# A mixture of experts in 26 units instead of 28: wide experts share a unit with a narrow one

## The chip, the cores and the metric

The kernel runs on one core of a Trainium2 chip. The metric is the time of one execution on the device in microseconds, the median of several runs. The engines are named as the profile names them: PE is the matrix engine TensorE (PEld its weight loads), DVE is VectorE, ACT is ScalarE, POOL is GpSimd, and SP is the engine whose queue issues nearly all DMAs here.

## The reference

Two transformer blocks run one after the other on 256 tokens of width 1024. The first has a pooling mixer, an attention layer and two dense feed-forward layers; the second has a gated recurrent mixer and then a mixture of 64 experts. The change concerns the mixture and, in one detail, the dense feed-forward layers.

```python
def moe_ffn(h, w_router, b_router, w_gu, w_down, w_sh_gu, w_sh_down):
    scores = jax.nn.sigmoid((h @ w_router).astype(jnp.float32))
    sel = scores + b_router
    ...                                   # keep the best 4 of 8 groups of experts
    _, top_e = lax.top_k(sel, TOP_K)      # 8 experts for each of 256 tokens
    w = jnp.take_along_axis(scores, top_e, axis=1)
    w = w / jnp.sum(w, axis=-1, keepdims=True) * ROUTED_SCALE
    ...
    out = swiglu_2(h_pad[tok], w_gu[e], w_down[e])   # per expert, on its own tokens
    acc = acc.at[tok].add(out * wts[:, None])
    ...
    return acc[:N] + swiglu_2(h, w_sh_gu, w_sh_down)
```

An expert is a gate-and-up product (1024 to 2 x 256), a SiLU gate, and a down product (256 to 1024), all in float32. 256 tokens times 8 choices are 2048 token slots over 64 experts; how many each expert gets depends on the data.

## The kernel before

**Weights.** An expert's weights are three pieces of 128 x 2048 float32 (1024 KB): the gate and up rows of the first and of the second half of the 1024 inputs, and the down rows. `load_experts` issues them on SP, L1735, for all experts of a unit piece by piece: first pieces of every expert, then second, then third. The pieces live in a ring of 17 buffers (`NEX` = 11 and `NEX2` = 6). A load waits until the matmuls have read what its buffer held before. Before the routed experts SP also loads three pieces of the shared expert.

**Units.** The core computes experts in units. A unit fills the 128 columns of TensorE's stationary operand with token slots, and the string `UNITS` gives the order:

```python
NFIX = 8
UNITS = "FFFFSSMHMSMMHMSMMHMSMMMHSMMM"
ROOM = {"F": (2, 64), "H": (1, 128), "M": (2, 64), "S": (4, 32)}
```

An F unit holds two given experts (the last eight by number, 56 to 63), with 64 slots each. The other 56 experts are ranked by their number of tokens: the 4 largest get an H unit each with 128 slots, the next 28 share 14 M units with 64 slots each, the 24 smallest share 6 S units with 32 slots each. The position in the string is the position in time. An expert with more tokens than slots has the rest done in a loop at the end (L1910), two entries at a time.

**The plan.** F units need no routing result for their loads, since their experts are given. For the others `placement` computes on the core which expert has which rank and writes the numbers into a small table, `plan` (L1644). SP reads the numbers of a unit's experts from it (`entry`, L1741), one read for each expert, and only then issues that unit's loads. `load_unit` and `loads` only set the order in SP's queue. The table has one column for each block of slots, `NCOL` = 60 in all.

**A unit's work.** For two neighbouring units `gather` (L1792) multiplies the tokens by a 0/1 matrix made by `onehot`; its result `xg` holds the units' tokens as columns. `front` (L1809) runs over the 8 blocks of 128 inputs, and for each over the experts of the unit; each expert has its own strip of output rows. Its first four blocks read the first piece of each expert, the last four the second. SiLU on ACT (L1812) and the product on DVE (L1814) follow. `back` (L1841) transposes the result and multiplies it by the third piece, in two halves of 512 columns; for each half it takes two steps. `scatter` (L1853) adds the unit's result to the accumulators of the tokens; it stands in the middle of the next unit, between front and back. So a unit frees its buffers at three steps: the middle of the front, the end of the front, the end of the back. Every float32 matmul is two instructions in the trace.

**Small buffers.** The dense feed-forward layers compute their gate in `swiglu`: ACT writes `sil` (L694), DVE multiplies it into `a32`, named `a` in the trace (L696), ACT makes the high part `ah` (L699), and POOL the low part `al` (L700). `sil` and `a32` have two buffers each, and the experts use the same.

Of the kernel before, what the change touches and what calls it, by code (L numbers as in the profile page):

```python
# [20 lines left out]
T = 256  # L21
# [6 lines left out]
NLIST = 32  # L28
NEX = 11
NEX2 = 6  # L30
NFIX = 8
UNITS = "FFFFSSMHMSMMHMSMMHMSMMMHSMMM"
ROOM = {"F": (2, 64), "H": (1, 128), "M": (2, 64), "S": (4, 32)}
NUNIT = len(UNITS)


def column_plan():


    count = {k: UNITS.count(k) * ROOM[k][0] for k in "HMS"}  # L40
    assert sum(count.values()) == N_EX - NFIX and 2 * UNITS[:NFIX // 2].count("F") == NFIX
    at = {"H": 0, "M": count["H"], "S": count["H"] + count["M"]}
    cols, first = [], []
    for k in UNITS[NFIX // 2:]:
        first.append(len(cols))
        for _ in range(ROOM[k][0]):
            cols.extend((at[k], s) for s in range(0, ROOM[k][1], 64))
            at[k] += 1
    return cols, first, count["H"], count["H"] + count["M"]


COLS, FIRST_COL, RANK_M, RANK_S = column_plan()
NCOL = len(COLS)


# [93 lines left out]
class Kern:  # L149
# [540 lines left out]

    def swiglu(self, ps):
        nc = self.nc
        sil = self.small([128, 256], "sil", 2)
        nc.scalar.activation(sil, ps[:, 0:256], AF.Silu)  # L694
        a = self.small([128, 256], "a32", 2)
        nc.vector.tensor_tensor(a, sil, ps[:, 256:512], op=ALU.mult)  # L696
        ah = self.small([128, 1, 256], "ah", TAIL + 1, F32R)
        al = self.small([128, 1, 256], "al", TAIL + 1, F32R)
        nc.scalar.copy(ah[:, 0, :], a)  # L699
        nc.gpsimd.tensor_tensor(al[:, 0, :], a, ah[:, 0, :], op=ALU.subtract)  # L700
        return ah, al
# [201 lines left out]
    def second_ffn(self, p):  # L903
# [11 lines left out]
        def load_x():  # L915
            for c in range(2):
                nc.gpsimd.dma_start(out=cx[:, c, :], in_=A["ctx"][128 * c:128 * c + 128, :])
            self.lower = self.small([128, 128], "lower", 1)
            nc.gpsimd.dma_start(out=self.lower, in_=A["lower"])

        def load_gs():
# [485 lines left out]
    def post(self, ctx, ws_ctx):  # L1407
# [20 lines left out]
        nc.gpsimd.dma_start(out=self.tri8, in_=self.A["tri8"])  # L1428
        self.ei = self.small([64, 4], "ei", 1)
        nc.gpsimd.dma_start(out=self.ei, in_=self.A["eidx"])  # L1430
        self.at = self.small([128, 128], "lower", 1)
        nc.gpsimd.dma_start(out=self.at, in_=self.A["colat"])
        self.loads(3 + NEX - 4)
        hs = [slice(512 * h, 512 * h + 512) for h in range(2)]
# [154 lines left out]
    def shared_expert(self):  # L1589

        nc, w, gu = self.nc, self.wsh, self.gu
        sil, act, aT = [], [], []
        for c in range(2):
            sil.append(self.small([128, 256], "sil", 2))
            nc.scalar.activation(sil[c], gu[c][:, 0:256], AF.Silu)
        for c in range(2):
            act.append(self.small([128, 256], "a32", 2))
            nc.vector.tensor_tensor(act[c], sil[c], gu[c][:, 256:512], op=ALU.mult)
        yield
        for c in range(2):  # L1600
# [12 lines left out]
        self.down = down  # L1613
        yield

    def placement(self):
# [4 lines left out]
        tmp = _Arena(self.small([128, 512], "hx", 3))  # L1621
        t = lambda n: tmp.tile([64, n])
        idx, given, key0 = ei[:, 0:1], ei[:, 2:3], ei[:, 3:4]
        ranks, bases = self.at[0:64, 0:NCOL], self.at[0:64, 64:64 + NCOL]
        n = N_EX - NFIX
        pc = self.pst([64, n + 1])
        for c in range(2):
# [16 lines left out]
        V.tensor_copy(self.plan, pe)  # L1644

        room, less = t(1), t(1)
        V.tensor_scalar(room, rank, RANK_M - 0.5, -64.0, op0=ALU.is_lt, op1=ALU.mult)
        V.tensor_scalar(less, rank, RANK_S - 0.5, 32.0, op0=ALU.is_gt, op1=ALU.mult)
        V.tensor_tensor(less, less, given, op=ALU.mult)
        V.scalar_tensor_tensor(room, room, -64.0, less, op0=ALU.add, op1=ALU.add)  # L1650
# [68 lines left out]
    def load_unit(self, n):  # L1719

        u = n - NFIX // 2
        if u < 0:
            idx = [N_EX - NFIX + 2 * n + e for e in range(2)]
        else:
            idx = self.entry(self.plan, FIRST_COL[u], ROOM[UNITS[n]][0])
        self.ex[n] = [[] for _ in idx]
        yield from self.load_experts(idx, self.ex[n])

# [31 lines left out]
    def experts(self):  # L1760
# [37 lines left out]
                    nc.vector.tensor_copy(xg[:, k0:k0 + 2, 0:m], ps[:, :, 0:m])  # L1798
            return xg, ow

        def front(ws, xg, j, inside={}):

            r, o = 128 // len(ws), 128 * j
            gu = self.psw()
            for k in range(8):
                for f in inside.get(k, ()):
                    f()
                for e, w in enumerate(ws):
                    nc.tensor.matmul(gu[r * e:r * e + r, :], xg[:, k, o + r * e:o + r * e + r],  # L1809
                                     w[k // 4][:, 512 * (k % 4):512 * (k % 4) + 512], start=(k == 0), stop=(k == 7))  # L1810
            sil = self.small([128, 256], "sil", 2)
            nc.scalar.activation(sil, gu[:, 0:256], AF.Silu)  # L1812
            act = self.small([128, 256], "a32", 2)
            nc.vector.tensor_tensor(act, sil, gu[:, 256:512], op=ALU.mult)  # L1814
            return act

        def back(ws, act, ow, j, scatter=lambda c, nb: None):

            r = 128 // len(ws)
# [12 lines left out]
            oT = self.small([128, 2, 128], "ah", TAIL + 1, F32R)  # L1832
            nc.vector.reduce_sum(sw, pt, axis=AX.X)
            nc.vector.tensor_scalar(oT.rearrange("p c t -> p (c t)"), pt, 0.0, None, op0=ALU.is_gt)
            yh = self.per.tile([128, 1024], F32R, tag="acc8", name="yh")
            yl = self.small([128, 1024], "grow", 3, F32R)
            for nb in range(2):
                y = self.psw()
                for f in range(2):
                    for e, w in enumerate(ws):  # L1840
                        nc.tensor.matmul(y[r * e:r * e + r, :], aT[:, f, r * e:r * e + r],  # L1841
                                         w[2][:, 1024 * f + 512 * nb:1024 * f + 512 * nb + 512],
                                         start=(f == 0), stop=(f == 1))
# [45 lines left out]
        for n in range(NUNIT):  # L1889
            ws = self.ex.pop(n)  # L1890
            done += 3 * len(ws)
            if n % 2 == 0:
                grp = gather(*oh, 2)
            act = front(ws, grp[0], n % 2, {} if n else {1: [lambda: next(self.shared)], 3: [lambda: next(side)],
                                                           6: [lambda: next(side)]})
            if n == 0:
                GP2 = self.row(self.rows, 7 * 1024, 1024)
# [4 lines left out]
            pend = scatter(*back(ws, act, grp[1], n % 2, pend))  # L1902
            next(side, None)
            if n == 0:
                self.down(1, 0)
# [5 lines left out]
        with tc.For_i(0, n, 2) as i:  # L1911
            ws = [[], []]
            for _ in self.load_experts(self.entry(self.li, i, 2), ws):
                pass
            grp = gather(*onehot([(self.slotx[:, :, ds(i, 2)], self.Wx[:, :, ds(i, 2)])]), 1)
            all4(scatter(*back(ws, front(ws, grp[0], 0), grp[1], 0)))
# [46 lines left out]
def _prepare(I):  # L1963
# [112 lines left out]
    at = np.zeros((128, 128), f32)  # L2076
    at[:, 0:NCOL] = [r for r, _ in COLS]
    at[:, 64:64 + NCOL] = [-s for _, s in COLS]
    A["colat"] = at
    A["eidx"] = ei  # L2080
    return A
# [14 lines left out]
```

## Time and profile before

| | us |
|---|---|
| median of 3 runs | 1332.54 (1332.06 to 1334.05) |
| the profiled execution, its own time | 1334.75 |
| span of its instructions | 1332.9 |
| PE busy | 1274.2 |
| DVE busy | 646.2 |
| ACT busy | 526.0 |
| POOL busy | 228.3 |

The experts are the last third of the span: their first front starts at 857.0 us. The busy time of PE is an upper figure, since matmuls overlap and their ends are modelled. All loads of expert weights go through one DMA queue, so the moved GB/s in a window and the times at which SP issues its loads say more about a limit there than a share of busy time does.

### The profile page before, as it was taken

The page shows a single profiled execution, that of the slowest core. Times are in us where ns is not written, and L with a number is a line of the kernel's source. Part 1 is how long each engine was busy: PE and PEld are TensorE (multiplying, and loading weights), DVE is VectorE, ACT ScalarE, POOL GpSimd, SP SyncE. Part 2 cuts the span into 40 slices and gives each one's busy share as a digit, 9 for nine tenths or more (in the row PEclk, how much of TensorE's full clock was granted, in tenths as well). Part 3 has the DMA queues.
Part 4 walks back from the last instruction along what each step waited for, and adds up shares of the span by engine and source line. Part 5 has one row for each costly group of instructions (what it writes and reads, how often), then busy time and mean ns, then how long its engine had stood idle before and what let it go on. Part 6 is the DMA issues. An engine that isn't in the chain of part 4 may idle for free. (4 is left out here: it accounts for less than half of the span.)

```text
span 1332.9 us, 20200 instructions
## 1 busy us (share of the span) xinstructions
PE 1274.2 (96%) x7812; PEld 922.1 (69%) x7812; DVE 646.2 (48%) x984; ACT 526.0 (39%) x883; POOL 228.3 (17%) x230
## 2 busy tenths in 40 slices
PE   7999999999999999989988899999998999999986
PEld 5889887988798998878887897544453443534532
DVE  5664555846657456576879557423222222222223
ACT  6534444557554456556645345311111111111112
POOL 1111112123033000125246442200000000000000
PEclk8999999999999999999999999999999999999998
DMA  8768678444485575646434478799999999999994
GB/s 301 252 231 280 248 270 316 155 164 159 130 326 189 189 249 194 221 151 242 143 104 136 152 274 342 273 372 378 405 420 420 419 420 419 420 419 420 421 420 192
DMA packets 72817, 374.45 MB, mean 281 GB/s; under 512 B 8932, under 2 KB 9364, under 8 KB 44304
## 3 DMA queue, kind: packets, MB, share of 16 engines
q1 hardware_dynamic: 68912, 361.25, 71.3%
q0 software_dynamic: 3664, 11.89, 2.8%
q8 instruction: 62, 1.02, 0.3%
q14 instruction: 35, 0.29, 0.1%
q10 hardware_dynamic: 144, 0.01, 0.0%
HBM read 371.99 MB, written 1.11 MB: 280 GB/s over the span
## 5 line engine op out<-in xcount | busy, mean ns | idle before, releaser
L137 DVE TENSOR_TENSOR wlo<-wland,whi 128x1024 fp32r<-128x1024 f32 x201 | 244.2, 1249 | 104.4 <-ACT whi L134 103.6
L258 PE MATMUL pw<-hT,whi 128*128 128x256 f32 x1856 | 250.6, 282 | 0.0
L134 ACT CAST whi<-wland 128x1024 fp32r<-128x1024 f32 x236 | 237.2, 1046 | 25.2 <-PE pa L267 12.7
L258 PEld LDWEIGHTS pw<-hT,whi 128*128 128x128 f32 x1856 | 232.9, 189 | 12.6 <-ACT whi L134 6.5
L1809 PE MATMUL pw<-ex,xg 128*64 128x512 f32 (+2 forms) x1024 | 208.5, 596 | 5.0 <-DMA ex<-ex 4.8
L1809 PEld LDWEIGHTS pw<-ex,xg 128*64 128x64 f32 (+2 forms) x1024 | 65.7, 130 | 133.3 <-issue 107.4
L258 PE MATMUL pw<-hT,wlo 128*128 128x256 f32 x928 | 128.2, 280 | 0.0
L1841 PE MATMUL pw<-ex,al 128*64 128x512 f32 (+2 forms) x512 | 113.2, 613 | 7.9 <-DMA ex<-ex 7.9
L258 PEld LDWEIGHTS pw<-hT,wlo 128*128 128x128 f32 x928 | 117.2, 189 | 0.2 <-POOL wlo L137 0.2
L137 POOL TENSOR_TENSOR wlo<-wland,whi 128x1024 fp32r<-128x1024 f32 x35 | 87.4, 2497 | 162.7 <-ACT whi L134 127.9
L267 PE MATMUL pa<-whi,hT 128*128 128x512 f32 x352 | 114.6, 401 | 0.0
L1814 DVE TENSOR_TENSOR a<-sil,pw 128x256 f32<-128x256 f32 x28 | 11.8, 421 | 190.5 <-ACT sil L1812 190.5
L1846 DVE SCALAR_TENSOR_TENSOR grow<-pw,sw,yh 128x512 fp32r<-128x512 f32 x56 | 42.1, 751 | 111.9 <-ACT yh L1845 111.0
L1812 ACT ACTIVATE sil<-pw 128x256 f32<-128x256 f32 x28 | 10.8, 385 | 209.0 <-PE pw L1809 209.0
L700 POOL TENSOR_TENSOR al<-a,ah 128x256 fp32r<-128x256 f32 x44 | 32.6, 742 | 326.9 <-ACT ah L699 326.9
L1841 PEld LDWEIGHTS pw<-ex,al 128*64 128x64 f32 (+2 forms) x512 | 31.9, 132 | 74.9 <-issue 49.9
L1845 ACT ACTIVATE yh<-pw,sw 128x512 fp32r<-128x512 f32 x56 | 38.5, 688 | 111.1 <-PE pw L1841 111.1
L694 ACT ACTIVATE sil<-pw 128x256 f32<-128x256 f32 x44 | 16.9, 384 | 164.7 <-PE pw L258 164.7
L1780 POOL TENSOR_TENSOR grow<-hx,Wp 128x256 f32<-128x256 f32 x24 | 14.7, 630 | 383.7 <-DVE hx L1778 383.7
L267 PEld LDWEIGHTS pa<-whi,hT 128*128 128x128 f32 x352 | 66.5, 189 | 16.1 <-DVE hT L248 0.4
L267 PE MATMUL pa<-wlo,hT 128*128 128x512 f32 x176 | 70.2, 399 | 5.0 <-DVE wlo L137 3.4
L267 PE MATMUL pa<-wlo,ah 128*128 128x512 f32 x176 | 69.8, 397 | 0.5 <-DVE wlo L137 0.5
(400 smaller groups left out, 1780.8 us busy)
## 6 DMA issues: line engine op xcount, KB each, us to landing
ex<-ex SPq DMA_DIRECT2D x192, 1024.0 KB
wland<-wd SPq DMA_DIRECT2D x236, 512.0 KB
ada<-ada SPq DMA_DIRECT2D x24, 1024.0 KB
row<-rows POOLq DMA_DIRECT2D x6, 512.0 KB, 4.9
ex<-exs SPq DMA_DIRECT2D x3, 1024.0 KB
bias<-bscr POOLq DMA_DIRECT2D x4, 512.0 KB, 4.8
x<-x SPq DMA_DIRECT2D x4, 256.0 KB
pw<-poolw SPq DMA_DIRECT2D x2, 512.0 KB
```

The costliest lines, as they stand in the source:

```text
L134: nc.scalar.copy(h, t)
L137: eng.tensor_tensor(l, t, h, op=ALU.subtract)
L258: self.nc.tensor.matmul(out, a[:, o:o + 128], b[:, k, :], start=(p == 0 and k == 0), stop=(p == 2 and k == nk - 1))
L267: self.nc.tensor.matmul(out, a[:, k, cs], b[:, lo:lo + n], start=(first and p == 0), stop=(last and p == 2))
L694: nc.scalar.activation(sil, ps[:, 0:256], AF.Silu)
L700: nc.gpsimd.tensor_tensor(al[:, 0, :], a, ah[:, 0, :], op=ALU.subtract)
L1780: nc.gpsimd.tensor_tensor(view(ow), view(oh), W[:, :, :, None].to_broadcast(shape), op=ALU.mult)
L1809: nc.tensor.matmul(gu[r * e:r * e + r, :], xg[:, k, o + r * e:o + r * e + r], w[k // 4][:, 512 * (k % 4):512 * (k % 4) + 512], start=(k == ...
L1814: nc.vector.tensor_tensor(act, sil, gu[:, 256:512], op=ALU.mult)
L1841: nc.tensor.matmul(y[r * e:r * e + r, :], aT[:, f, r * e:r * e + r], w[2][:, 1024 * f + 512 * nb:1024 * f + 512 * nb + 512], start=(f == 0 ...
L1845: nc.scalar.activation(yh[:, sl], y, AF.Copy, scale=sw)
L1846: nc.vector.scalar_tensor_tensor(yl[:, sl], y, sw, yh[:, sl], op0=ALU.mult, op1=ALU.subtract)
```

## The change

The 4 H units go, and there are 4 T units in their place. A T unit holds one of the 4 largest experts with 96 slots (L) and one small expert with 32 slots (S). With four small experts placed there, and six given experts and not eight, the string becomes 3 F, 6 S, 4 T and 13 M units: 26.

The 96 slots of an L expert are two strips, 64 and 32 columns wide, since a strip starts at a multiple of its width; `strips` lists them. So the front of a T unit has three matmuls for each of 8 blocks where H had one, and the back three for each of its 4 steps. The rooms are 96 for ranks 0 to 3, 64 for ranks 4 to 29 and 32 for the last 28 of 58 ranked experts.

The table of columns grows to `NCOL` = 66, and its tile from 128 to 132 columns. `sil` and `a32` have one buffer each and not two; the shared expert, which needs two at once, takes the second from `ah` and `al`.

```diff
-NFIX = 8
-UNITS = "FFFFSSMHMSMMHMSMMHMSMMMHSMMM"
-ROOM = {"F": (2, 64), "H": (1, 128), "M": (2, 64), "S": (4, 32)}
+NFIX = 6
+UNITS = "FFFSSTMMSTMMSTMMSTMMSMMMMM"
+ROOM = {"F": 64, "L": 96, "M": 64, "S": 32}
+PARTS = {"F": "FF", "M": "MM", "T": "LS", "S": "SSSS"}
...
+        for k in PARTS[u]:
+            own[-1].append(len(cols))
+            cols.extend((at[k], s) for s in range(0, ROOM[k], 64 if u == "M" else 32))
             at[k] += 1
...
+def strips(unit):
+    at, out = 0, []
+    for k in PARTS[unit]:
+        out.append([(at + s, min(64, ROOM[k] - s)) for s in range(0, ROOM[k], 64)])
+        at += ROOM[k]
+    return out
...
     def swiglu(self, ps):
-        sil = self.small([128, 256], "sil", 2)
+        sil = self.small([128, 256], "sil", 1)
-        a = self.small([128, 256], "a32", 2)
+        a = self.small([128, 256], "a32", 1)
...
-        self.at = self.small([128, 128], "lower", 1)
+        self.at = self.small([128, 2 * NCOL], "lower", 1)
...
-            sil.append(self.small([128, 256], "sil", 2))
+            sil.append(self.small([128, 256], ("sil", "ah")[c], (1, TAIL + 1)[c]))
-            act.append(self.small([128, 256], "a32", 2))
+            act.append(self.small([128, 256], ("a32", "al")[c], (1, TAIL + 1)[c]))
...
-        V.tensor_scalar(room, rank, RANK_M - 0.5, -64.0, op0=ALU.is_lt, op1=ALU.mult)
+        V.tensor_scalar(room, rank, RANK_M - 0.5, -32.0, op0=ALU.is_lt, op1=ALU.mult)
...
-            idx = self.entry(self.plan, FIRST_COL[u], ROOM[UNITS[n]][0])
+            idx = [x for c in OWN_COLS[u] for x in self.entry(self.plan, c, 1)]
...
-                for e, w in enumerate(ws):
-                    nc.tensor.matmul(gu[r * e:r * e + r, :], xg[:, k, o + r * e:o + r * e + r],
-                                     w[k // 4][:, 512 * (k % 4):512 * (k % 4) + 512], start=(k == 0), stop=(k == 7))
+                for w, own in zip(ws, strips(unit)):
+                    for s, r in own:
+                        nc.tensor.matmul(gu[s:s + r, :], xg[:, k, o + s:o + s + r],
+                                         w[k // 4][:, 512 * (k % 4):512 * (k % 4) + 512], start=(k == 0), stop=(k == 7))
...
-                    for e, w in enumerate(ws):
-                        nc.tensor.matmul(y[r * e:r * e + r, :], aT[:, f, r * e:r * e + r],
-                                         w[2][:, 1024 * f + 512 * nb:1024 * f + 512 * nb + 512],
-                                         start=(f == 0), stop=(f == 1))
+                    for w, own in zip(ws, strips(unit)):
+                        for s, r in own:
+                            nc.tensor.matmul(y[s:s + r, :], aT[:, f, s:s + r],
+                                             w[2][:, 1024 * f + 512 * nb:1024 * f + 512 * nb + 512],
+                                             start=(f == 0), stop=(f == 1))
```

Three places show what moves. The names are `out<-in` with the tile's shape; `ex` is a piece of an expert's weights. The first place is SP's queue at the end of the loads of given experts, before:

```order
L1735 DMA ex_8312<-ex 128x2048
L1735 DMA ex_8314<-ex 128x2048
L1735 DMA ex_8316<-ex 128x2048
L1735 DMA ex<-ex 128x2048 x11
L1741 TENSOR_LOAD plan
L1741 ISA x2
```

And the same place after the change:

```order
L1748 DMA ex_8312<-ex 128x2048
L1748 DMA ex_8314<-ex 128x2048
L1748 DMA ex_8316<-ex 128x2048
L1748 DMA ex<-ex 128x2048 x5
L1754 TENSOR_LOAD plan
L1754 ISA x2
```

The first of four reads of the plan moved ahead of six loads. The second place is PE at the fourth unit (position 3), before:

```order
L1841 MATMUL pw<-ex,al 64x512 x8
L1701 MATMUL pt<-hx,ei 1x32 x4
L1702 MATMUL pt<-hx,ei 1x1
L1667 MATMUL pt<-cst,sc 64x128 x2
L1809 MATMUL pw<-ex,xg 64x512 x16
```

And after:

```order
L1855 MATMUL pw<-ex,al 64x512 x8
L1714 MATMUL pt<-hx,ei 1x32 x4
L1715 MATMUL pt<-hx,ei 1x1
L1680 MATMUL pt<-cst,sc 64x128 x2
L1823 MATMUL pw<-ex,xg 32x512 x18
```

Where the last F unit had two strips of 64 (16 matmuls), an S unit with four strips of 32 now stands, with its 32 matmuls and twelve loads. The third place is PE at a front with one of the largest experts, before an H unit (position 7):

```order
L1853 MATMUL pa<-grow,ah 128x512
L1841 MATMUL pw<-ex,al 64x512 x8
L1809 MATMUL pw<-ex,xg 128x512 x8
L1853 MATMUL pa<-yh,ah 128x512
L1853 MATMUL pa<-grow,ah 128x512
```

And after, the start of the first T unit's front (position 5), where the last row begins the second block:

```order
L1855 MATMUL pw<-ex_8941,al 32x512
L1823 MATMUL pw<-ex_8963,xg 64x512
L1823 MATMUL pw<-ex_8963,xg 32x512
L1823 MATMUL pw<-ex_8965,xg 32x512
L1823 MATMUL pw<-ex_8963,xg 64x512
```

One matmul over 128 columns became three, over 64 and 32 columns of the large expert (`ex_8963`) and 32 of the small one (`ex_8965`).

## Rows read from the trace of the kernel before

**Rows 1.** The page: GB/s in 40 equal slices; DMA issues, count and size.

```profile
GB/s 301 252 231 280 248 270 316 155 164 159 130 326 189 189 249 194 221 151 242 143 104 136 152 274 342 273 372 378 405 420 420 419 420 419 420 419 420 421 420 192
...
ex<-ex SPq DMA_DIRECT2D x192, 1024.0 KB
```

**Rows 2.** Windows: us, busy (count) of PE, PEld, DVE, ACT, POOL; PEclk, DMA, GB/s.

```profile
898.00:902.00 4.00, 4.00 (x20) 1.29 (x18) 0.00 (x0) 0.00 (x0) 0.00 (x0) 1.00 0.70 225
...
914.00:918.00 4.00, 4.00 (x20) 1.21 (x16) 0.00 (x0) 0.06 (x1) 0.00 (x0) 1.00 0.99 348
918.00:922.00 4.00, 4.00 (x24) 2.91 (x25) 2.07 (x6) 0.69 (x2) 1.22 (x2) 1.00 0.98 377
...
930.00:934.00 4.00, 4.00 (x44) 1.26 (x40) 0.00 (x0) 0.00 (x0) 0.00 (x0) 1.00 0.96 338
934.00:938.00 4.00, 4.00 (x34) 2.01 (x27) 0.56 (x2) 0.38 (x1) 0.00 (x0) 1.00 0.86 350
...
900.00:945.00 45.00, 44.45 (x296) 20.46 (x296) 13.27 (x37) 8.19 (x16) 1.22 (x2) 1.00 0.97 380
945.00:1310.00 365.00, 352.15 (x1814) 162.09 (x1808) 81.55 (x154) 59.86 (x110) 13.44 (x22) 1.00 1.01 420
...
1104.00:1108.00 4.00, 4.00 (x24) 0.98 (x17) 0.00 (x0) 0.61 (x1) 0.00 (x0) 0.57 1.02 424
```

**Rows 3.** Timeline of PE, the last units: start, us, instruction, idle before and its releaser.

```profile
1280.33 3.65 PE L1809 MATMUL pw<-ex,xg 128*64 128x512 f32 x14 [1.33 <-DMA ex<-ex]
...
1289.99 4.16 PE L1792 MATMUL pt<-hx,h 128*128 128x256 f32 x32
1294.08 7.09 PE L1809 MATMUL pw<-ex,xg 128*64 128x512 f32 x32
...
1307.16 7.09 PE L1809 MATMUL pw<-ex,xg 128*64 128x512 f32 x32
...
1316.66 3.65 PE L1841 MATMUL pw<-ex,al 128*64 128x512 f32 x16
...
1320.24 0.51 PE L1853 MATMUL pa<-yh,ah 128*128 128x512 f32 x1
```

**Rows 4.** Timeline of PE: the front of an S unit and of an H unit.

```profile
929.16 7.07 PE L1809 MATMUL pw<-ex,xg 128*32 128x512 f32 x64
...
1060.06 7.03 PE L1809 MATMUL pw<-ex,xg 128*128 128x512 f32 x16
```

**Rows 5.** Timeline of PE: the first front, where 128 columns interrupt 64.

```profile
857.04 1.08 PE L1809 MATMUL pw<-ex,xg 128*64 128x512 f32 x4
858.05 0.66 PE L1603 MATMUL pt<-cst,a 128*128 128x128 f32 x4
```

**Rows 6.** Issues on SP: reads of the plan (ns, starts), then single expert loads.

```profile
L1741 SPq TENSOR_LOAD <-plan x4: 262/268/478, 882.3 to 884.3; - x4
...
865.70 0.33 SPq L1735 DMA_DIRECT2D ex<-ex  x1
881.96 0.33 SPq L1735 DMA_DIRECT2D ex<-ex  x1
885.10 0.35 SPq L1735 DMA_DIRECT2D ex<-ex  x1
899.72 0.33 SPq L1735 DMA_DIRECT2D ex<-ex  x1
...
949.14 0.33 SPq L1735 DMA_DIRECT2D ex<-ex  x1
1295.31 0.33 SPq L1735 DMA_DIRECT2D ex<-ex  x1
```

**Rows 7.** Timeline of DVE: the plan is written.

```profile
863.84 0.21 DVE L1644 CAST plan<-pt 1x60 int32<-1x60 f32 x1 [1.50 <-PE pt L1642]
```

**Rows 8.** Timelines of POOL and DVE in the first feed-forward layer.

```profile
39.46 0.74 POOL L700 TENSOR_TENSOR al<-a,ah 128x256 fp32r<-128x256 f32 x1 [4.13 <-ACT ah L699]
...
44.12 0.42 DVE L696 TENSOR_TENSOR a<-sil,pw 128x256 f32<-128x256 f32 x1 [0.17 <-ACT sil L694]
```

More of the change, by code (lines that the diff above doesn't have):

```diff
@@ L30 @@
 NEX2 = 6
-NFIX = 8
-UNITS = "FFFFSSMHMSMMHMSMMHMSMMMHSMMM"
-ROOM = {"F": (2, 64), "H": (1, 128), "M": (2, 64), "S": (4, 32)}
+NFIX = 6
+UNITS = "FFFSSTMMSTMMSTMMSTMMSMMMMM"
+ROOM = {"F": 64, "L": 96, "M": 64, "S": 32}
+PARTS = {"F": "FF", "M": "MM", "T": "LS", "S": "SSSS"}
 NUNIT = len(UNITS)
 def column_plan():
[L40 to L44, printed above, removed]
+    count = {k: sum(PARTS[u].count(k) for u in UNITS) for k in "FLMS"}
+    assert UNITS[:NFIX // 2] == "F" * (NFIX // 2) and count["F"] == NFIX and sum(count.values()) == N_EX
+    at = {"L": 0, "M": count["L"], "S": count["L"] + count["M"]}
+    cols, first, own = [], [], []
+    for u in UNITS[NFIX // 2:]:
         first.append(len(cols))
-        for _ in range(ROOM[k][0]):
-            cols.extend((at[k], s) for s in range(0, ROOM[k][1], 64))
+        own.append([])
+        for k in PARTS[u]:
+            own[-1].append(len(cols))
+            cols.extend((at[k], s) for s in range(0, ROOM[k], 64 if u == "M" else 32))
             at[k] += 1
-    return cols, first, count["H"], count["H"] + count["M"]
-COLS, FIRST_COL, RANK_M, RANK_S = column_plan()
+    return cols, first, own, count["L"], count["L"] + count["M"]
+def strips(unit):
[4 more added lines that the diff above has]
+    return out
+COLS, FIRST_COL, OWN_COLS, RANK_M, RANK_S = column_plan()
 NCOL = len(COLS)
@@ L917, in load_x @@
                 nc.gpsimd.dma_start(out=cx[:, c, :], in_=A["ctx"][128 * c:128 * c + 128, :])
-            self.lower = self.small([128, 128], "lower", 1)
+            self.lower = self.small([128, 2 * NCOL], "lower", 1)[:, 0:128]
             nc.gpsimd.dma_start(out=self.lower, in_=A["lower"])
@@ L1623, in placement @@
         idx, given, key0 = ei[:, 0:1], ei[:, 2:3], ei[:, 3:4]
-        ranks, bases = self.at[0:64, 0:NCOL], self.at[0:64, 64:64 + NCOL]
+        ranks, bases = self.at[0:64, 0:NCOL], self.at[0:64, NCOL:2 * NCOL]
         n = N_EX - NFIX
@@ L1799, in gather, with front @@
             return xg, ow
-        def front(ws, xg, j, inside={}):
-            r, o = 128 // len(ws), 128 * j
+        def front(ws, unit, xg, j, inside={}):
+            o = 128 * j
             gu = self.psw()
@@ L1807, in front, with back @@
                     f()
-                for e, w in enumerate(ws):
-                    nc.tensor.matmul(gu[r * e:r * e + r, :], xg[:, k, o + r * e:o + r * e + r],
-                                     w[k // 4][:, 512 * (k % 4):512 * (k % 4) + 512], start=(k == 0), stop=(k == 7))
-            sil = self.small([128, 256], "sil", 2)
+                for w, own in zip(ws, strips(unit)):
+                    for s, r in own:
+                        nc.tensor.matmul(gu[s:s + r, :], xg[:, k, o + s:o + s + r],
+                                         w[k // 4][:, 512 * (k % 4):512 * (k % 4) + 512], start=(k == 0), stop=(k == 7))
+            sil = self.small([128, 256], "sil", 1)
             nc.scalar.activation(sil, gu[:, 0:256], AF.Silu)
-            act = self.small([128, 256], "a32", 2)
+            act = self.small([128, 256], "a32", 1)
             nc.vector.tensor_tensor(act, sil, gu[:, 256:512], op=ALU.mult)
             return act
-        def back(ws, act, ow, j, scatter=lambda c, nb: None):
-            r = 128 // len(ws)
+        def back(ws, unit, act, ow, j, scatter=lambda c, nb: None):
             for c, nb in ((0, 0), (0, 1), (1, 0)):
@@ L1893, in experts @@
                 grp = gather(*oh, 2)
-            act = front(ws, grp[0], n % 2, {} if n else {1: [lambda: next(self.shared)], 3: [lambda: next(side)],
+            act = front(ws, UNITS[n], grp[0], n % 2, {} if n else {1: [lambda: next(self.shared)], 3: [lambda: next(side)],
                                                            6: [lambda: next(side)]})
@@ L1901, in experts @@
                 oh = onehot(two(n + 1))
-            pend = scatter(*back(ws, act, grp[1], n % 2, pend))
+            pend = scatter(*back(ws, UNITS[n], act, grp[1], n % 2, pend))
             next(side, None)
@@ L1915, in experts @@
             grp = gather(*onehot([(self.slotx[:, :, ds(i, 2)], self.Wx[:, :, ds(i, 2)])]), 1)
-            all4(scatter(*back(ws, front(ws, grp[0], 0), grp[1], 0)))
+            all4(scatter(*back(ws, "M", front(ws, "M", grp[0], 0), grp[1], 0)))
         self.warm(AF.Sqrt)
@@ L2075, in _prepare @@
     ei[:, 3] = -ei[:, 0] - 1.0e6 * (1.0 - ei[:, 2])
-    at = np.zeros((128, 128), f32)
+    at = np.zeros((128, 2 * NCOL), f32)
     at[:, 0:NCOL] = [r for r, _ in COLS]
-    at[:, 64:64 + NCOL] = [-s for _, s in COLS]
+    at[:, NCOL:] = [-s for _, s in COLS]
     A["colat"] = at
```

## The prediction, made before the changed kernel ran

> **What bounds the kernel now.** I began with the slices of the page. In the last third the moved bytes stand at 419 to 421 GB/s slice after slice, and the page lists 192 expert loads of 1024 KB, which is 64 experts times three [rows 1]. The windows say it more exactly: from 945 to 1310 us the queue moves 420 GB/s without a dip, while from 900 to 945 it moves 380 [rows 2]. One load of 1.049 MB at 420 GB/s is 2.50 us. The issue rows agree: from the load issued at 949.14 to the last one at 1295.31 there are 138 steps in 346.17 us, 2.51 us each [rows 6]. So from 945 us on, the weights bound the kernel, and both kernels load the same 192 pieces.
>
> Then the timeline of TensorE, for what a unit costs it. The last two M units run from the gather at 1289.99 to the scatter that follows them at 1320.24, 30.25 us for a pair (gather 4.16, twice front 7.09, scatter and transposes, back 3.65) [rows 3]. Twelve loads are 30.0 us. So TensorE keeps pace with M units almost exactly, and waits in S units (12 loads in one unit). Just after the last S it waits for a load (1.33 us before the row at 1280.33), and from there to the end it waits for none [rows 3].
>
> The time is therefore: the moment when the queue becomes saturated, plus a fixed amount of loading, plus the TensorE work after the last place where it waited for data. Only the first and the third can change.
>
> **The change, part by part.** The sum is made against the profiled execution: span 1332.9 us, its own time 1334.75; the median is 1332.54, and I apply the difference to that.
>
> *Two units fewer.* 28 units at 30.25/2 = 15.1 us become 26: TensorE has 30.25 us less to do. The loads it waits for cover that fully, so I count nothing. The cover goes only if a unit gets dearer (below).
>
> *The ring frees faster, earlier.* A load needs a place in a ring of 17 pieces, and before 945 us the queue is idle because TensorE has not yet freed places. An F unit frees two at each of its three steps, an S unit four. Position 3 was F and is S now; its releases at about 914, 918 and 925 us free 12 places, 30 us of loading, in place of 6. From 900 to 945 the idle share is 1 - 380/420, that is 4.3 us [rows 2]. Of this the row 914 to 918 gives 0.69 us (348 GB/s), 918 to 922 gives 0.41 (377), 930 to 934 gives 0.78 (338) and 934 to 938 gives 0.67 (350): 2.5 us that I expect to go. The row 898 to 902 (225 GB/s, 1.86 us) lies before the new releases and stays. What idles before 898 belongs to units 0 to 2, which are the same F units.
>
> *Reads of the plan move.* The first load of each routed unit is behind reads of its experts' numbers on SP: four reads, the first at 882.3 and the last at 884.3, stand between the load issued at 881.96 and the next at 885.10, 3.14 us apart where two that need nothing stand some 0.5 apart: 2.6 us [rows 6]. With six given experts these reads stand after 18 expert loads and not 24. The load that went out at 865.70 is now the first one behind them. The plan is written at 863.84, for 0.21 us [rows 7]; 864.05 plus 2.6 is 866.7, so this load is 1.0 us later, in a stretch where places in the ring set the pace. The place in the old order, at 882, loses its 2.6 us in turn. The next S unit has its reads behind the load of 899.72 [rows 6], and the one after it goes out up to 2.3 us later than it did; there the queue is nearly empty (225 GB/s), so this is new idle time. I take a third of it, 0.8, since four loads released by 903 and 910 queue up behind it and part of the lost time was idle anyway; the bounds are 0 and 2.3. Gain at the moment of saturation: 2.5 - 0.8 = **1.7 us**, between 0.2 and 3.4 (4.3 less the half of 1.86 that lies after 900).
>
> *The four T units.* H was one expert with 128 columns, 8 matmuls in the front and 4 in the back. T does 64, 32 and 32 columns as three, so 24 and 12. The trace has no unit of mixed widths. It has three of one width: one 128 strip takes 7.03 us for a front, two 64 strips 7.09, four 32 strips 7.07 [rows 3, 4]. Strips of one width overlap wholly, and the nearest rows say that T costs 7.1 too: nothing extra. The other bound is no overlap: three strips one after the other cost twice more, 2 x (7.09 + 3.65) = 21.5 us, and each change of width something. A change from 64 to 128 columns shows: from four instructions of a 64 pair to the next width it is 1.01 us (857.04 to 858.05), against 4/32 of 7.09 = 0.89 in a steady front [rows 3, 5], 0.12 more. With 24 changes (16 in the front, 8 in the back) that is 2.9, in all 24.4. Between them: the 64 strip alone, the two 32 strips together, 10.7 + 2.9 = 13.6 us. I take 0, but the result is the same up to 14.5: a stretch S T M M has 30 loads, 75.0 us, and four units of TensorE, 60.5. What a T costs below 14.5 us extra goes into waiting that is there anyway.
>
> On this the Trainium skill speaks against the change: its page TensorEngine Tiling (Array Packing), Key Properties, says that changing the tiling mode, and not just the tile, drains TensorE. By that rule the widths would not overlap and the middle or upper case would hold, and the sum would stay as it is or be that of the slower rival; no row before shows widths side by side.
>
> *The end.* After the last S there were three M units and now there are five. In each pair TensorE needs 30.25 and the loads 30.0, so the lag grows by one more 0.25, say **+0.3 us**. That the first of them waits for data as now is what carries this step. Longer waits in S units can lower TensorE's clock: in one S unit that had waited for its loads the granted clock was 0.57 from 1104 to 1108 [rows 2], mostly the lower of its two levels (1.2 and 2.4 GHz). About 4 us at half speed cost 2; where loads are waited for anyway it costs nothing, at the very end up to 2.
>
> *One buffer for sil and a32.* In the first FFN the POOL subtraction that reads a32 runs 39.46 to 40.20, and the next write of a32 starts at 44.12 [rows 8], 3.9 us later, the closest pair of the trace. So the new wait is met already and costs nothing. The wider table, 66 columns and not 60, adds a few columns to instructions of 0.2 us; nothing waits for them.
>
> Sum: -1.7 + 0.3 = -1.4 us, **1331.1 us** against 1332.54, which is -0.1%.
>
> **Rivals.**
> *Slower: widths do not overlap at all.* T costs 24.4 us extra, 9.9 over the cover of 14.5, in four units 40 us: 1371 us. It decides from 14.5 us per T, so also the middle case with changes twice as dear (10.7 + 5.8 = 16.5, four times 2.0) gives 1339. For it: the 64 strip and the 32 strips are of different shape, and a boundary costs something even now [rows 5]. Against it: strips of one width run side by side without loss [rows 3, 4], and the middle case at the seen price stays under the cover. Chance 0.12.
>
> *Faster: 3 us or more of the idle time after 900 us goes.* If all 4.3 goes and the reads cost nothing, the time is 1332.54 - 4.3 + 0.3 = 1328.5. Against it: the places for the loads around 900 are freed by units 0 to 2, which do not change. Chance 0.11.
>
> *It does not do what it says:* an expert has more tokens than its room, and the loop for overflow runs: six loads with nothing ahead, 15 us, and a gather, front, scatter and back of 17, so some 32 us, 1363. The router's formula on the reference's inputs gives 73, 73, 61, 58, 56 for the largest of the 58 ranked experts and 29 for the 31st, against rooms of 96, 64 and 32. Chance 0.02.
>
> **How the numbers follow.** The forecast has 0.75. About 0.2%, 2.7 us, is what a measurement of this kernel can tell from no change; the forecast lies within it. Faster by more is the second rival, 0.11; slower by more is the first and the third, 0.14; within it 0.75. The range of the forecast itself is 1329.9 (gain 2.9; more is the second rival) to 1334.6 (gain 0.2, +0.3, a clock loss of 2). For 8 in 10 I reach from the faster rival's 1328.5 to 1335.5, just past the point where a T unit begins to show; above it lie 0.12 or so, below it a few hundredths.
>
> **What would show it.** Right: 420 GB/s from about 920 us on, a gap of some 2.6 us in the issues behind the load at 899.7, fronts of T at most 17 us, several us of waiting for loads in each S unit, no wait after the first of the five last M units. Wrong: windows under 420 GB/s after a T unit, T fronts over 18 us and no waits in S units (the slow rival), issues in the loop for overflow, or 420 GB/s already from 900.

## The result and the profile after

| | before | after |
|---|---|---|
| median, same session | 1333.62 us (1332.06 to 1335.80) | 1343.14 us (1339.43 to 1343.24) |
| ratio, 95% interval | | 1.0062 [1.0051, 1.0074] |
| profiled span | 1332.9 us | 1341.5 us |

The changed kernel is slower by 0.6%, some 9 us, where no difference was forecast; 1343.14 lies outside the range. The stage that the prediction is about did not do it. The timeline of PE after the change, first front of the experts and last back:

```profile
866.59 1.08 PE L1823 MATMUL pw<-ex,xg 128*64 128x512 f32 x4
...
1325.27 3.65 PE L1855 MATMUL pw<-ex,al 128*64 128x512 f32 x16
```

From the one to the other it is 458.68 us; before it was 1316.66 - 857.04 = 459.62 [rows 3, 5]. So the experts take 0.9 us **less**. The first front starts at 866.59 where it started at 857.04: the 9.55 us are lost **ahead of the experts**, in code of which the change touches only the number of two small buffers and the width of small tables.

Where, the groups of the page by cost tell. They are sorted by busy time; the number behind it is the mean ns of one instruction, and the last is idle time ahead of the group. Before:

```profile
L258 PE MATMUL pw<-hT,whi 128*128 128x256 f32 x1856 | 250.6, 282 | 0.0
```

and after, the same line of the helper `fm` (now L271):

```profile
L271 PE MATMUL pw<-hT,whi 128*128 128x256 f32 x1856 | 255.8, 285 | 0.0
L271 PE MATMUL pw<-hT,wlo 128*128 128x256 f32 x928 | 130.8, 283 | 0.0
```

The same count, no idle time in either, and each instruction some ns longer. 2112 of the 2784 are the gate and up products of the two dense feed-forward layers; the other 672 are products of the attention and of the recurrent mixer that go through the same helper. In all of them 128 x 128 blocks of the streamed weights (`whi`, `wlo`) are stationary and 256 columns of the tokens (`hT`) move. Overlapped durations are a poor measure; the distance between starts is a better one. Two rows of the timeline of PE before,

```profile
67.97 2.03 PE L258 MATMUL pw<-hT,whi 128*128 128x256 f32 x16
69.84 1.09 PE L258 MATMUL pw<-hT,wlo 128*128 128x256 f32 x8
```

and two after:

```profile
70.97 2.08 PE L271 MATMUL pw<-hT,whi 128*128 128x256 f32 x16
72.89 1.12 PE L271 MATMUL pw<-hT,wlo 128*128 128x256 f32 x8
```

Sixteen instructions take 1.87 us before and 1.92 after: 117 and 120 ns each. As a mean over the neighbours in these two groups that follow each other without a pause (under 150 ns from start to start), worked out from the starts in the trace, it is 116.9 and 119.9 ns. 2784 instructions times 3.0 ns are 8.4 us, if no wait takes up any of it.

Not all of the 9.55 us is this. The rows above are 3.0 us late already, behind only 208 of the 2784, and there the clock differs: 0.72 from 30 to 40 us after the change, a mix of its two levels (1.2 and 2.4 GHz), where it was 1.00 before. In the 30 us ahead of that PE was busy for 21.6 us after and 21.7 before, so its work does not tell the two apart. Windows from 30 to 40 us (us, PE busy and count, granted clock, DMA share, GB/s), before and then after:

```profile
30.00:40.00 10.00, 9.96 (x82) 1.00 0.33 104
30.00:40.00 10.00, 9.97 (x61) 0.72 0.28 81
```

The mean granted clock of the whole profile hides it: 0.988 before and 0.987 after. From 40 to 560 us it is 1.00 in both, and there the lag grows without help from the clock. These are the last gate and up products of the second dense layer, before and after:

```profile
575.51 1.09 PE L258 MATMUL pw<-hT,whi 128*128 128x256 f32 x8
583.31 1.12 PE L271 MATMUL pw<-hT,whi 128*128 128x256 f32 x8
```

They are 7.8 us late, so 4.8 us came in between, with 2088 of the instructions. The last 1.75 us come behind that, where the clock falls for some us at a time in both (a mean of 0.98 before and 0.97 after from 560 to 850 us). Over all runs the clock is a small part: the mean is 0.9870 in the 6 runs of after and 0.9880 in the 26 runs of before beside e1, and 0.001 of 1340 us is 1.3 us.

The windows of the expert stage after the change (us, busy and count of PE, PEld, DVE, ACT, POOL, granted clock, DMA share, GB/s), to be held against those from 900 to 945 and from 945 to 1310 in [rows 2]:

```profile
910.00:955.00 45.00, 44.45 (x326) 19.76 (x322) 13.28 (x37) 8.19 (x16) 1.22 (x2) 1.00 1.00 399
955.00:1318.00 363.00, 360.27 (x1813) 143.83 (x1814) 74.14 (x140) 54.42 (x100) 12.22 (x20) 1.00 1.01 420
```

They begin 10 us later, as the stage does: the same 420 GB/s without a dip, and 399 in place of 380 on the way there. And the front and back of the first T unit on PE:

```profile
952.36 15.95 PE L1823 MATMUL pw<-ex,xg 128*64 128x512 f32 x48
...
970.75 8.01 PE L1855 MATMUL pw<-ex,al 128*64 128x512 f32 x24
```

15.95 us in place of 7.09 and 8.01 in place of 3.65: a T unit costs 13.2 us more than an M unit.

### The profile page after: what moved, and what is told of

Its sections match the earlier page's. It is cut to its first block, busy times and chain, and to the rows that moved or that the text cites. A ratio compares the mean times of both kernels' runs of the same rounds, so it can differ in the third digit from the quotient of the medians.

```text
span 1341.5 us, 20295 instructions
## 1 busy us (share of the span) xinstructions
PE 1294.6 (97%) x7852; PEld 913.4 (68%) x7852; DVE 638.3 (48%) x970; ACT 520.7 (39%) x873; POOL 226.8 (17%) x228
## 5 line engine op out<-in xcount | busy, mean ns | idle before, releaser
L271 PE MATMUL pw<-hT,whi 128*128 128x256 f32 x1856 | 255.8, 285 | 0.0
L271 PEld LDWEIGHTS pw<-hT,whi 128*128 128x128 f32 x1856 | 237.8, 190 | 13.3 <-ACT whi L147 6.5
L1823 PE MATMUL pw<-ex,xg 128*64 128x512 f32 (+1 forms) x1088 | 222.5, 597 | 2.4 <-DMA ex<-ex 2.4
L1823 PEld LDWEIGHTS pw<-ex,xg 128*64 128x64 f32 (+1 forms) x1088 | 58.5, 124 | 152.5 <-issue 136.8
L271 PE MATMUL pw<-hT,wlo 128*128 128x256 f32 x928 | 130.8, 283 | 0.0
L271 PEld LDWEIGHTS pw<-hT,wlo 128*128 128x128 f32 x928 | 119.8, 189 | 0.1
L1855 PE MATMUL pw<-ex,al 128*64 128x512 f32 (+1 forms) x544 | 115.2, 599 | 0.4 <-DMA ex<-ex 0.4
L1860 DVE SCALAR_TENSOR_TENSOR grow<-pw,sw,yh 128x512 fp32r<-128x512 f32 x52 | 39.0, 751 | 107.8 <-ACT yh L1859 107.8
L1855 PEld LDWEIGHTS pw<-ex,al 128*64 128x64 f32 (+1 forms) x544 | 28.5, 123 | 73.8 <-issue 62.2
L1859 ACT ACTIVATE yh<-pw,sw 128x512 fp32r<-128x512 f32 x52 | 35.7, 687 | 107.1 <-PE pw L1855 107.1
L280 PE MATMUL pa<-whi,al 128*128 128x512 f32 x176 | 69.7, 396 | 0.0
```

The costliest lines, as they stand in the source:

```text
L271: self.nc.tensor.matmul(out, a[:, o:o + 128], b[:, k, :], start=(p == 0 and k == 0), stop=(p == 2 and k == nk - 1))
L280: self.nc.tensor.matmul(out, a[:, k, cs], b[:, lo:lo + n], start=(first and p == 0), stop=(last and p == 2))
L1823: nc.tensor.matmul(gu[s:s + r, :], xg[:, k, o + s:o + s + r], w[k // 4][:, 512 * (k % 4):512 * (k % 4) + 512], start=(k == 0), stop=(k == 7))
L1855: nc.tensor.matmul(y[s:s + r, :], aT[:, f, s:s + r], w[2][:, 1024 * f + 512 * nb:1024 * f + 512 * nb + 512], start=(f == 0), stop=(f == 1))
```

## The experiments

**The theory.** What the dense layers execute is the same, so only where it lies can differ. `sil` and `a32` with one buffer each free 2048 bytes per partition, and the wider tables take 192. All that is allocated behind them moves down, the pool of the streamed weights by 1856 bytes: the first `whi` tile lies at 102304 before and at 100448 after, while `hT` stays at 51904 (addresses in bytes per partition, of the built programs). The theory is that this move, and not the units, costs the 9 us. The rivals: the units or the waits on the single buffers cost them. Two kernels part these.

**e1_pad1856.** The changed kernel, with an unused tile of 1856 bytes ahead of the weight pool, so that the pool lies where it lay before.

```diff
         self.Wx = self.small([128, 2, NLIST], "Wx", 1)
+        self.small([128, 464], "pad", 1)
```

> The changed kernel with one unused tile of 1856 bytes at the end of the persistent pool, so that the streamed weights (whi, wlo) and the expert ring stand at the same SBUF addresses as in the kernel before; units, strips and the single sil and a32 buffers stay as changed. Address theory (the stage before the experts is slower because the weights moved by 1856 bytes): the 128x256 matmuls of the feed-forward layers are 117 ns apart again, not 120.5, the first expert front starts at 857 us and not 866.6, time 1332 to 1333. Buffer theory (the single sil and a32 cost it): still 1341 to 1343. Run theory (it is a state of the chip): before and this differ by less than 2 us and both scatter.

**e2_before_low.** The 28 units of before, with single buffers as in the change and 192 bytes more, so that the pool lies where the change puts it.

```diff
-        sil = self.small([128, 256], "sil", 2)
+        sil = self.small([128, 256], "sil", 1)
...
-        a = self.small([128, 256], "a32", 2)
+        a = self.small([128, 256], "a32", 1)
...
         self.Wx = self.small([128, 2, NLIST], "Wx", 1)
+        self.small([128, 48], "pad", 1)
```

> The kernel before with its 28 units, and of the change only sil and a32 with one buffer each (the shared expert takes its second from ah and al), plus an unused tile of 192 bytes, so that the streamed weights stand at the addresses of the changed kernel (1856 bytes lower). Address theory: 8 to 10 us slower than before, 1342 to 1344, 128x256 matmuls 120.5 ns apart. Unit theory (the 26 units are what costs): as before, 1333. Buffer theory: also slower by 8 to 10; the run with the larger unused tile tells these two apart.

Measured: e1 1331.62 us, ratio 0.9986 [0.9972, 1.0001]; e2 1341.96, ratio 1.0057 [1.0039, 1.0075]. The loss follows the address and not the units. On PE, first e1 and then e2, the same rows of the dense layer and the first front:

```profile
65.75 2.03 PE L271 MATMUL pw<-hT,whi 128*128 128x256 f32 x16
67.61 1.09 PE L271 MATMUL pw<-hT,wlo 128*128 128x256 f32 x8
...
854.38 1.08 PE L1824 MATMUL pw<-ex,xg 128*64 128x512 f32 x4
...
1312.41 3.65 PE L1856 MATMUL pw<-ex,al 128*64 128x512 f32 x16
```

```profile
67.94 1.22 PE L258 MATMUL pw<-hT,whi 128*128 128x256 f32 x8
69.00 1.12 PE L258 MATMUL pw<-hT,wlo 128*128 128x256 f32 x8
...
865.41 1.08 PE L1810 MATMUL pw<-ex,xg 128*64 128x512 f32 x4
...
1325.57 3.65 PE L1842 MATMUL pw<-ex,al 128*64 128x512 f32 x16
```

In e1 sixteen take 1.86 us, where it was 1.87 before; in e2 a step of eight is 1.12 us long, as after (1.09 in e1), and the first front is 8.4 us later than before, with all of before's units. e1 has the single buffers too and reaches the first front no later than before (854.38 against 857.04), so their waits cost nothing there.

**Which addresses?** e3_pad32 and e4_pad64 move the pool of the changed kernel up by 32 and 64 bytes; e7_pad160 and e8_pad224 by 160 and 224 (these two ran once). The edit is the line of e1 with another number (8, 16, 40 or 56 words).

> The changed kernel with an unused tile of 32 bytes, which puts the streamed weights and the expert ring 32 bytes higher, on a multiple of 128 bytes (100480 for the first whi tile). Address theory with alignment as its rule: 128x256 matmuls at 117 ns or less, time 1332 or less. If the rule is the distance between the two operands and not the alignment: anything from 113 to 121 ns, time 1325 to 1343. Buffer theory: 1341 to 1343.

> The same with 64 bytes: the first whi tile at 100512, which has the same place within 128 and 256 bytes as in the kernel before (102304), but another within 512. Address theory: 117 ns and 1332 if only the place within 128 or 256 bytes counts; 119 to 121 ns and 1340 to 1343 if a larger stride does. Buffer theory: 1341 to 1343.

> The changed kernel with an unused tile of 160 bytes: first whi tile at 100608, on a multiple of 256 bytes. So far the distance between 128x256 matmuls is 117.0 ns at places 160 within 256, 117.6 at 128, 119.4 at 96. If alignment to 256 is best: 113 to 116 ns and 1318 to 1330. If the place relative to the other operand (hT, at 192 within 256) decides: 117 to 120 ns, 1332 to 1342.

> The same with 224 bytes: first whi tile at 64 within 256. If the price follows the place within 256 smoothly (96 was dearest so far): 118 to 121 ns, 1338 to 1345. If only places 32 to 64 bytes off a multiple of 128 cost: 117 ns and 1332.

Measured: 1334.92 us (ratio 1.0008 [0.9998, 1.0018]), 1333.02 (0.9992 [0.9979, 1.0004]), 1321.31 and 1334.38. 64 bytes are enough to undo the loss, so the distance of 1856 means nothing; and with 160 there is a kernel some 12 us faster than before.

**e9_before_aligned and e10_after_aligned.** That place, timed, for both sets of units. e10 is e7 again; e9 is e2 with 96 bytes in place of 192, so that `whi` starts at a multiple of 256.

```diff
         self.Wx = self.small([128, 2, NLIST], "Wx", 1)
+        self.small([128, 24], "pad", 1)
```

> The kernel before with its 28 units, sil and a32 with one buffer each as in the change, and an unused tile of 96 bytes that puts the first whi tile on a multiple of 256 bytes (100352). Address theory: 128x256 matmuls 115.1 ns apart, 10 to 12 us faster than before, 1321 to 1324, in the other order of units too. If the gain at that address belonged to the 26 units: 1331 to 1334.

> The changed kernel with the unused tile of 160 bytes again, now timed: 1319 to 1323, and 1 to 3 us under the 28 units at an aligned address, which is the worth of the units alone (1.4 us was forecast). If the units are worth nothing: equal within 0.5 us.

Measured: e9 1323.66 us, ratio 0.9922 [0.9905, 0.9939]; e10 1322.06, ratio 0.9915 [0.9896, 0.9934]. Both are faster than both kernels, and e10 has the lowest median of all kernels that ran more than once. Its rows on PE:

```profile
66.94 1.98 PE L271 MATMUL pw<-hT,whi 128*128 128x256 f32 x16
68.75 1.07 PE L271 MATMUL pw<-hT,wlo 128*128 128x256 f32 x8
...
847.41 1.08 PE L1824 MATMUL pw<-ex,xg 128*64 128x512 f32 x4
...
1302.67 3.65 PE L1856 MATMUL pw<-ex,al 128*64 128x512 f32 x16
```

Sixteen take 1.81 us here, 113 ns each.

**e11_hT_aligned and e12_both_moved.** Is it where the weights lie by themselves, or how far they lie from the other operand? In both kernels `hT` moves up by 64 bytes, to a multiple of 256. In e11 `whi` lies as in e10, at a multiple of 256; in e12 it moves 64 bytes up as well, so that the distance is that of e10.

```diff
             cst = per.tile([128, 3 * 128 + 66], F32, tag="cst", name="cst")
+            self.small([128, 16], "pad0", 1)
...
         self.Wx = self.small([128, 2, NLIST], "Wx", 1)
+        self.small([128, 24], "pad", 1)
```

e12 has 40 in place of 24.

> As the run before, but the moving operand hT also stands on a multiple of 256 bytes (51968 and not 51904, by an unused tile of 64 bytes ahead of it and 96 behind). If each operand's own alignment counts: under 115 ns and 1 to 5 us faster than the run before. If only the stationary operand's place counts: the same 115.1 ns and the same time. If the distance between the two counts (it changes by 64 bytes): 115 to 119 ns, up to 12 us slower.

> The changed kernel with hT on a multiple of 256 bytes (51968) and the first whi tile 64 bytes past one (100672): both operands moved together by 64 bytes against the fast run, so each one's own place is one at which a slow run stood (whi at 64: 118.6 ns; hT at 0: 119.6 ns), and the distance is that of the fast run. Distance theory (the price hangs on whi minus hT within 256 bytes): 115.1 ns, 1320 to 1324. Own-place theory: 118 to 120 ns, 1333 to 1343.

Measured: e11 1333.02 us, ratio 0.9992 [0.9982, 1.0002]; e12 1323.74, ratio 0.9915 [0.9895, 0.9935]. The rows on PE, e11 and then e12:

```profile
70.12 2.08 PE L271 MATMUL pw<-hT,whi 128*128 128x256 f32 x16
72.04 1.12 PE L271 MATMUL pw<-hT,wlo 128*128 128x256 f32 x8
...
860.82 1.08 PE L1825 MATMUL pw<-ex,xg 128*64 128x512 f32 x4
```

```profile
68.08 1.98 PE L271 MATMUL pw<-hT,whi 128*128 128x256 f32 x16
69.89 1.07 PE L271 MATMUL pw<-hT,wlo 128*128 128x256 f32 x8
...
848.41 1.08 PE L1825 MATMUL pw<-ex,xg 128*64 128x512 f32 x4
```

The best place of the weights is no good with `hT` 64 bytes further, and the next place is good when `hT` moves along. So it is the **distance** of the two operands, as far as two places of `hT` can show it. Nor does it take another engine or a DMA: among the neighbours during which DVE, ACT and POOL all stood idle (519 before, 531 after) the mean spacing is 116.9 and 120.1 ns, and among those during which no DMA packet was under way (493 and 564) it is 117.0 and 119.9. All kernels by distance, with the mean spacing worked out as above:

| `whi` - `hT`, modulo 256 bytes | kernels | mean spacing, ns | first front, us |
|---|---|---|---|
| 64 | e7, e9, e10, e12 | 114.1 to 115.0 | 847.4 to 848.4 |
| 224 | before, e1, e4, e5, e6 | 116.9 | 854.4 to 857.0 |
| 192 | e3 | 117.6 | 858.4 |
| 128 | e8 | 118.7 | 858.3 |
| 160 | after, e2 | 119.9 | 865.4 and 866.6 |
| 0 | e11 | 119.9 | 860.8 |

The distances 32 and 96 were not run. e11 has the spacing of after and yet reaches the experts 5.8 us sooner. That sits in the matmuls over 512 columns ahead of the experts (line of `tm`, 1056 instructions with `hT`, `ah` and `al`): without pauses (under 300 ns) their mean spacing is 233.9 ns after and 228.7 in e11, which makes 5.5 us. It is 229.2 to 229.7 in e7, e9, e10 and e12, and 232.3 to 233.9 in all others. So they are faster in all kernels with `whi` at a multiple of 256, and in e12 too; what decides there was not parted.

**The T units.** e5_grouped (on top of e1) runs in a T unit first all matmuls of the 64 strip and then those of the two 32 strips, in front and back. e6_twice (on top of e1) runs the 64 strip's part of a T front once more ahead of it; the second pass starts the sums anew.

```diff
+def parts(ws, unit):
+    every = [(w, s, r) for w, own in zip(ws, strips(unit)) for s, r in own]
+    wide = [x for x in every if x[2] == 64]
+    slim = [x for x in every if x[2] == 32]
+    return [wide, slim] if unit == "T" else [every]
...
-            for k in range(8):
+            for k, part in [(k, part) for part in parts(ws, unit) for k in range(8)]:
```

In e6 the last line of `parts` gives `[wide, every]`.

> The changed kernel with the unused tile of 1856 bytes (weights at the old addresses); in T units all matmuls of the 64 strip come first, then those of the two 32 strips, so a front has one change of width in place of 15, a back two in place of 7 or so. If unequal widths do not overlap and each change costs 0.11 us (front 15.95 us in the changed kernel): front 14.2 to 14.4, back 7.3 to 7.5. If they overlapped in part: front below 14 before and no gain now. Cover theory (what a T costs under 14.5 us extra is hidden): time as with the tile of 1856 bytes alone, 1331.6 within 1.5, and more waiting for loads in the S units. No cover: 4 x 2.2 us faster, 1323.

> As with the tile of 1856 bytes, but each T front runs the 64 strip's eight matmuls once more ahead of the usual order (the second pass starts its sum anew, so the result is unchanged): 7.1 us more, T 20.3 us dearer than an M unit. Cover theory: 20.3 is 5.8 over the cover of 14.5, four times, so 1331.6 + 23 = 1355, between 1350 and 1359, and the loads drop under 420 GB/s behind T units. All of it counts: 1331.6 + 28 = 1360. None counts: 1332.

Measured: e5 1331.80 us, ratio 0.9993 [0.9979, 1.0006]; e6 1352.51, ratio 1.0148 [1.0126, 1.0170]. The front and back of the first T on PE, in e5 and in e6, and of e6 the first front and the last back:

```profile
941.26 14.07 PE L1831 MATMUL pw<-ex,xg 128*64 128x512 f32 x48
...
957.75 7.47 PE L1862 MATMUL pw<-ex,al 128*64 128x512 f32 x24
```

```profile
856.97 1.08 PE L1831 MATMUL pw<-ex,xg 128*64 128x512 f32 x4
...
942.77 22.82 PE L1831 MATMUL pw<-ex,xg 128*64 128x512 f32 x64
...
1335.34 3.65 PE L1863 MATMUL pw<-ex,al 128*64 128x512 f32 x16
```

14.07 us is twice the 7.03 that one strip takes alone [rows 4]: the 64 strip and the pair of 32 strips each take a full pass and share nothing. Interleaved, the front changes width 15 times and grouped once; 15.95 - 14.07 over 14 changes is 0.13 us each. The time does not follow: e5 is as fast as e1. In e6 a front is 6.87 us longer, 27.5 for four, and the expert stage is 1335.34 - 856.97 = 478.37 us, 20.3 more than the 458.03 of e1. 7.2 us of 27.5 were hidden, 1.8 per T, so the cover was 13.2 + 1.8 = 15.0 us per T. What PE waits for expert loads says the same: 7.9 + 4.8 = 12.7 us in all before, 2.4 + 0.4 = 2.8 after, 5.1 + 3.7 = 8.8 in e5 with its cheaper T units, and nothing in e6. That cover is spent shows in the windows too; e6, to be held against the 420 above:

```profile
910.00:1310.00 400.00, 400.00 (x2067) 159.09 (x2066) 79.41 (x158) 57.97 (x108) 13.45 (x22) 1.00 1.00 408
```

## Why the prediction was wrong, by its steps

**The failed step: "One buffer for sil and a32 … costs nothing".** It asked whether the new wait is met, and it is: e1 has it and is not slower. It did not ask what the freed 2048 bytes do to everything allocated behind. They moved the stationary operand of 2784 matmuls against the moving one, from 116.9 to 119.9 ns each, up to 8.4 us, in layers that the sum left out as unchanged. Moving the weights back by padding takes the loss away (e1, e4), and the same move with the units of before brings it (e2). The early fall of the clock, some 2.4 us in the profile of after (3.0 us of lag less 208 times 3.0 ns), is in no term either; whether it hangs on the addresses is open. No row of before shows this price, but that two operands move against each other could be read off the change, and it should have been bounded like any unseen cost. The sign came out as in the slower rivals, and the cause is in none of them: a T costs less than the cover, and the loop for overflow did not run.

**The units by themselves: right.** With `whi` at equal places the 26 units gain 1.9 us by the ratio (before to e1, interval -3.7 to +0.1), 1.6 us (e9 to e10) and lose 1.2 us (e2 to after, timed in different sessions); the medians can't tell these from nothing. The trace is sharper: from the first front to the start of the last back it is 459.62 us before and 458.03 in e1 (-1.6), 460.16 in e2 and 458.68 after (-1.5), 457.19 in e9 and 455.26 in e10 (-1.9). Forecast was -1.4. e9's ends are these two rows:

```profile
848.39 1.08 PE L1810 MATMUL pw<-ex,xg 128*64 128x512 f32 x4
...
1305.58 3.65 PE L1842 MATMUL pw<-ex,al 128*64 128x512 f32 x16
```

**The ring and the plan reads: right.** Issues on SP in e1 (start, us, count), and its windows that answer to 900 to 945 and 945 to 1310 of [rows 2]:

```profile
897.08 0.33 SPq L1749 DMA_DIRECT2D ex<-ex  x1
...
899.94 0.33 SPq L1749 DMA_DIRECT2D ex<-ex  x1
...
944.25 0.33 SPq L1749 DMA_DIRECT2D ex<-ex  x1
```

```profile
897.30:942.30 45.00, 44.45 (x327) 19.91 (x324) 13.28 (x37) 8.18 (x16) 1.22 (x2) 1.00 0.99 395
942.30:1307.00 364.70, 362.12 (x1822) 145.30 (x1823) 74.10 (x140) 54.34 (x100) 12.20 (x20) 1.00 1.01 420
```

The load at 944.25 is the same one in order as that of 949.14 [rows 6]. It goes out 89.87 us after the first front, where it went out 92.10 us after it: 2.2 us gained, against 1.7; by the same two rows it is 1.8 from e2 to after and 1.2 from e9 to e10. The forecast gap behind the reads (some 2.6 us behind the load issued at 899.7) is there: 2.86 us behind 897.08.

**The T units: the value 0 was wrong, the result of it right.** The term lay between 0 and 24.4; measured 13.2 is the middle case of 13.6, with a change of width at 0.13 us where 0.12 had been read off [rows 5]. The prediction leaned to the nearest rows, which all had strips of one width. What saved the sum is the cover, 14.5 forecast and some 15.0 by e6. The Trainium skill, TensorEngine Tiling (Array Packing), Key Properties, says that a change of tiling mode drains TensorE; the traces of after and e5 agree, with 13.2 us per T and 0.13 us per change.

**The end: +0.3 forecast, not confirmed.** From that load to the start of the last back it is 1316.66 - 949.14 = 367.52 us before [rows 3, 6] and 368.16 in e1, +0.6; but +0.3 from e2 to after and -0.8 from e9 to e10, so a term of this size is not shown. That S units would wait several us each did not come true, since T units ate the cover; after the change PE waits for loads around the last S alone:

```profile
1237.24 7.07 PE L1823 MATMUL pw<-ex,xg 128*32 128x512 f32 x64
...
1247.97 3.62 PE L1855 MATMUL pw<-ex,al 128*32 128x512 f32 x26 [0.16 <-DMA ex<-ex]
...
1252.94 3.65 PE L1823 MATMUL pw<-ex,xg 128*64 128x512 f32 x16 [0.35 <-DMA ex<-ex]
...
1258.61 3.65 PE L1823 MATMUL pw<-ex,xg 128*64 128x512 f32 x14 [2.02 <-DMA ex<-ex]
```

After the first of the five last M units there is no wait, as forecast.

## What to carry to other kernels

A change to the size or number of a small buffer moves every tile behind it: list the addresses of the operands of the busiest matmuls before and after, and if their distance changes, bound that cost over their whole count. When a result goes against the forecast, compare the start of the changed stage first; if it starts late, what is to be explained lies ahead of it. And hold addresses fixed with a dummy tile, and read the granted clock window by window, before judging such a change, since 26 units and 28 differ here by under 2 us while 64 bytes of padding move the changed kernel by 10.

## What the runs showed of the hardware

**The spacing of back-to-back matmuls depends on the distance of their two operands in SBUF.** Over 256 moving columns with a new stationary block for each it was 114.1 to 119.9 ns, by the distance modulo 256 bytes; before and after, most of these matmuls ran from 40 to 560 us, at a granted clock of 1.00. Why is open: a collision of the read of the next stationary block with that of the moving columns would fit, but it was only argued. `wlo` moved along with `whi` in every kernel and starts at the same place modulo 256. The Trainium skill, SBUF — State Buffer, Who interferes with whom, says that PE never waits on another engine; the trace agrees, with 120.1 ns after the change where DVE, ACT and POOL stood idle and 119.9 where at least one worked. The same section calls TensorE's two reads, of the moving columns and of the weights, independent; by that no distance between them should matter, and here it does by 5.8 ns, so the measurement decides.

**Loads may be faster at a multiple of 256 bytes.** Six of the 17 buffers of the expert ring lie in a pool that is opened where the pool of the streamed weights stood, and start at the same place modulo 256 as `whi` in every kernel. The four kernels where these start at a multiple of 256 (e7, e9, e10, e11) load at 423 GB/s from 950 to 1290 us; the other kernels but e6 load at 420. First e10, then e12, whose pool lies 64 bytes higher:

```profile
950.00:1290.00 340.00, 338.47 (x1744) 139.44 (x1744) 72.28 (x138) 52.64 (x97) 12.22 (x20) 1.00 1.01 423
```

```profile
950.00:1290.00 340.00, 337.39 (x1732) 138.18 (x1732) 71.43 (x135) 52.23 (x96) 12.21 (x20) 1.00 1.01 420
```

0.7% of the 365 us of saturated loading is 2.6 us, and the expert stage of e10 is 458.03 - 455.26 = 2.8 us shorter than that of e1. With 28 units, where PE waits 12.0 us for loads, e9 is 459.62 - 457.19 = 2.4 us shorter than before, which a faster PE alone would hardly give. The tile `xg` moved along too, and no run parts its share. The other 11 buffers lay at 224 modulo 256 in all kernels; moving them was not tried.
